# VectorE's sums of weight blocks, tied behind the remainder of the second pair of weights ahead of them

## The chip, the cores and the metric

The kernel runs on one core of a Trainium2 chip. Its time is device microseconds (us) of that core for one execution; the median of several runs counts. In the texts below, PE is TensorE (matmuls), DVE is VectorE, ACT is ScalarE, POOL is GpSimd and SP is SyncE, whose queue issues most of the loads.

## The reference, cut to what matters

Two transformer blocks over 256 rows of 2048 float32 numbers. The first has a mixer (gated linear attention and dilated attention), and then the gated feed-forward layer in which the change lies:

```
h2 = rms_norm(x, norm2_g)
x = x + (silu(h2 @ w_gate) * (h2 @ w_up)) @ w_down      # w_gate, w_up: 2048 x 5632; w_down: 5632 x 2048
```

The second block has retention, a convolution and windowed attention, each with large projections. Nearly all of the work is matmuls of the 256 rows with weight matrices that are read from memory once.

## The kernel before, in words

**Products in three parts.** Each float32 operand is split into a rounded part `hi` (a cast on ACT, line 168) and the remainder `lo` = source - `hi` (a subtraction on DVE, line 169). The helper `split` writes both. A product is then three matmuls (`three`, lines 193 to 195): x hi with w hi, x hi with w lo, x lo with w hi.

**Weights.** `linear` walks over one 512-column slice of a matrix. A `raw` tile holds 2 x 128 rows of it (128 x 1024 numbers, 512 KB), loaded by SP (`rows`, line 126) into one of 5 buffers. `split` makes a *pair* (`hi`, `lo`) of it in one of 4 buffers, and twelve matmuls use the pair. A cast can start when PE is through with the pair four before it; a load can start when the remainder of the raw tile five before it is done.

**The feed-forward layer.** The 5632 hidden columns are 11 slices of 512. Six of them are `plain`: gate product, tanh, up product, then line 562 (DVE) multiplies gate and up, and `act_done` transposes the result on PE (line 551). The other five are computed by `seven`: a 2 x 2 block product with seven multiplications in place of eight. I call each such slice a *block of products*; its work is cut into 28 pieces, which stand in the queue `side`. `deal`, called after each group of three matmuls of a `linear`, takes a piece from that queue every 1.75 groups (the first 12 pieces) or 5.75 groups (the other 16). So the pieces lie between the matmuls of `plain` and `down`.

**The sums.** Each of the last 16 pieces of a block (`rest`) takes four blocks of weights b12, b11, b22, b21 (tiles named `b` or `u`, in a ring of six; loaded by `ahead` one group of four pieces early), makes a sum of two of them in place (a subtraction on DVE, line 676, 128 x 1024), splits the sum into a pair by `parts` and multiplies it by `times` (six matmuls). Five blocks have 80 sums. b12 - b11 is written over b11, b12 - b22 over b12, b22 - (b12 - b11) over b22, and b21 - that over b21.

**What sets the order.** Each engine works through its own queue in order. The order in a queue is made when the program is built, by a scheduler with its own estimate of when each instruction can run (`schedule_with_timeline_sim=True`). Where its estimate has a block of weights landed, it puts the sum into DVE's queue at the first free place.

Of the kernel before, what the change touches and what calls it, by code (L numbers as in the profile page):

```python
# [9 lines left out]
F32 = mybir.dt.float32  # L10
# [3 lines left out]
ALU = mybir.AluOpType  # L14
# [66 lines left out]
def model(ctx, tc, a, out):  # L81
# [12 lines left out]
    V, A, G, T = nc.vector, nc.scalar, nc.gpsimd, nc.tensor  # L94
    cnt = [0]

    def nm(s):
        cnt[0] += 1
        return f"{s}{cnt[0]}"
# [4 lines left out]
    def unit(i, shape, dtype=F32):  # L104
        return wk.tile([P] + list(shape), dtype, tag=f"u{i}", name=nm(f"u{i}_"))
# [15 lines left out]
    def raw_tile():  # L121
        return raw_p.tile([P, 2, 512], F32, tag="raw", name=nm("raw"))

    def rows(dst, w, k, c0, n=512):

        return nc.sync.dma_start(dst[:, :, :n], w[k * P:(k + 2) * P, c0:c0 + n].rearrange("(k p) f -> p k f", p=P))

    def fetch(w, kg, c0, n):

        raws = [raw_tile() for _ in range(2)]  # L130
        for i in range(2):
            rows(raws[i], w, 4 * kg + 2 * i, c0, n)
        return raws
# [29 lines left out]
        G.tensor_tensor(o, ms, nhalf[:, :ms.shape[-1]], ALU.pow)  # L163


    def split(hi, lo, src, scale=None):
        if scale is None:
            A.copy(hi, src)  # L168
            V.tensor_tensor(lo, src, hi.bitcast(F32), ALU.subtract)  # L169
        else:  # L170
            A.activation(hi, src, AF.Copy, scale=scale)
            V.scalar_tensor_tensor(lo, src, scale, hi.bitcast(F32), ALU.mult, ALU.subtract)
# [12 lines left out]
    def deal():  # L185
        if side:
            pace[1] += 1
            if pace[1] >= pace[0]:
                pace[1] -= pace[0]
                side.popleft()()  # L190

    def three(o, xh, xl, hi, lo, start, stop):
        T.matmul(o, xh, hi, start=start, stop=False)  # L193
        T.matmul(o, xh, lo, start=False, stop=False)  # L194
        T.matmul(o, xl, hi, start=False, stop=stop)  # L195

    def linear(w, c0, n, groups, got=(), fine=False):
        accs = [ps_acc.tile([P, 512], F32, tag="acc", name=nm("acc")) for _ in range(2)]
        for gi, ((xh, xl), kg) in enumerate(groups):
            raws = got[gi] if gi < len(got) else fetch(w, kg, c0, n)  # L200
            for k in range(4):
                k2 = k % 2
                if k2 == 0:
                    raw = raws[k // 2]
                    hi = hl_p.tile([P, 2, 512], F32R, tag="hi", name=nm("hi"))
                    lo = hl_p.tile([P, 2, 512], F32R, tag="lo", name=nm("lo"))
                    if fine and gi == 0:
                        for j in range(2):
                            split(hi[:, j, :n], lo[:, j, :n], raw[:, j, :n])
                    else:  # L210
                        split(hi[:, :, :n], lo[:, :, :n], raw[:, :, :n])
                for t in range(2):
                    o = accs[t][:, :n]
                    st, en = gi == 0 and k == 0, gi == len(groups) - 1 and k == 3
                    sl = slice(t * P, (t + 1) * P)
                    three(o, xh[:, k, sl], xl[:, k, sl], hi[:, k2, :n], lo[:, k2, :n], st, en)
                    deal()
        return accs
# [82 lines left out]
    def silu_gate(dst, acc, rh_t):  # L301

        A.activation(dst, acc, AF.Tanh, scale=rh_t)
        V.scalar_tensor_tensor(dst, dst, 1.0, acc, ALU.add, ALU.mult)
# [127 lines left out]
    for vb in range(2):  # L432
# [4 lines left out]
        for hh in range(2):  # L437
# [19 lines left out]
            for t in range(2):  # L457
                o = po[:, t * S:(t + 1) * S]
                T.matmul(o, aT[:, t], v[:, t, vs], start=True, stop=True)
                for c in range(2):  # L460
                    n = 2 * t + c
# [82 lines left out]
    def act_done(j, sg):  # L544
        ah, al = acts[j] = pair(mt_p, "m")
        for i in range(2):
            ps = ps_w.tile([P, 512], F32, tag="w", name=nm("tr"))
            for k in range(2):
                for t in range(2):
                    c = (2 * i + k) * P  # L550
                    T.transpose(ps[:, k * S + t * P:k * S + (t + 1) * P], sg[:, t, c:c + P], ident)
            split(ah[:, 2 * i:2 * i + 2].rearrange("p c s -> p (c s)"),
                  al[:, 2 * i:2 * i + 2].rearrange("p c s -> p (c s)"), ps)
# [50 lines left out]
    def parts(src):  # L604
        hi = hl_p.tile([P, 2, 512], F32R, tag="hi", name=nm("hi"))
        lo = hl_p.tile([P, 2, 512], F32R, tag="lo", name=nm("lo"))
        split(hi, lo, src)
        return hi, lo

    def times(o, which, hl, kp):  # L610
        for j in range(2):
            k = 2 * kp + j
            three(o, *left(which, k), hl[0][:, j], hl[1][:, j], k == 0, k == 7)

    def temp(tag, bufs):
        return sm.tile([P, 512], F32, tag=tag, name=nm("c"), bufs=bufs)
# [3 lines left out]
    def block_tile():  # L620

        i = ring[0] % 6
        ring[0] += 1
        if i < 2:
            return raw_p.tile([P, 2, 512], F32, tag=f"b{i}", name=nm("b"), bufs=1)
        if i < 4:
            return mt_p.tile([P, 2, 512], F32, tag="n" + "hl"[i - 2], name=nm("b"), bufs=1)
        return unit(6 + i, [2, 512])

    def work_bank():  # L630
        return ps_w.tile([P, 512], F32, tag="w", name=nm("at"))

    def seven(j):

        c0 = j * 512
        c = {}

        def first(kp, n):
            if kp == 0:
                c[n] = work_bank()  # L640
            raw = raw_tile()
            rows(raw, (w_gate, w_up, w_gate)[n], (0, 8, 8)[n] + 2 * kp, c0)
            times(c[n], ("A11", "S4", "A12")[n], parts(raw), kp)
            if n == 2:
                ahead(0, kp)
            if kp < 3:
                return
            if n < 2:
                c["p", n] = temp("Lx", 4)
                A.copy(c["p", n], c[n])  # L650
                return
            sg = c["sg"] = unit(5, [2, 512])
            c11 = temp("junk2", 3)
            V.tensor_tensor(c11, c["p", 0], c[2], ALU.add)
            silu_gate(sg[:, 0], c11, rh[:, 0:1])

        def ahead(kp, n):

            if kp > 3:
                return  # L660
            for i in ((0, 1), (), (2,), (3,))[n]:
                b = c["b", kp, i] = block_tile()
                load = rows(b, (w_up, w_gate, w_up, w_gate)[i], (0, 0, 8, 8)[i] + 2 * kp, c0)
                if j == 1 and kp == 0:
                    tc.keep_in_program_order(load)

        def rest(kp, n):
            ahead(kp + 1, n)
            if n == 0:
                if kp == 0:  # L670
                    pace[0] = 5.75
                    c["P"] = [work_bank() for _ in range(3)] + [ps_acc.tile([P, 512], F32, tag="acc", name=nm("acc"))]
            b12, b11, b22, b21 = [c["b", kp, i] for i in range(4)]
            dst, x0, x1, which = ((b11, b12, b11, "S1"), (b12, b22, b12, "S3"), (b22, b22, b11, "S2"),
                                  (b21, b22, b21, "A22"))[n]
            V.tensor_tensor(dst, x0, x1, ALU.subtract)  # L676
            times(c["P"][n], which, parts(dst), kp)
            if kp == 3 and n == 3:
                last()

        def last():
            b5, b7, b6, b4 = c["P"]
            p1, p3, sg = c["p", 0], c["p", 1], c["sg"]
            V.tensor_tensor(p1, p1, b6, ALU.add)
            c12, c21 = temp("junk2", 3), temp("junk2", 3)
            V.tensor_tensor(c12, p1, b5, ALU.add)
            V.tensor_tensor(p1, p1, b7, ALU.add)
            V.tensor_tensor(c21, p1, b4, ALU.subtract)
            V.tensor_tensor(p1, p1, b5, ALU.add)
            V.tensor_tensor(c12, c12, p3, ALU.add)  # L690
            silu_gate(sg[:, 1], c21, rh[:, 1:2])
            for t, cu in enumerate((c12, p1)):
                V.scalar_tensor_tensor(sg[:, t], cu, r2h[:, t:t + 1], sg[:, t], ALU.mult, ALU.mult)
            act_done(j, sg)


        pace[0] = 1.75
        side.extend([lambda kp=kp, n=n: first(kp, n) for kp in range(4) for n in range(2)])
        side.extend([lambda kp=kp: first(kp, 2) for kp in range(4)])
        side.extend([lambda kp=kp, n=n: rest(kp, n) for kp in range(4) for n in range(4)])  # L700

    def drain():
# [369 lines left out]
```

## Time and profile before

| | us |
|---|---|
| median of 3 runs (lowest, highest) | 1926.29 (1925.13, 1928.86) |
| the profiled execution | 1927.01 |
| its span, first to last instruction | 1924.9 |
| PE busy | 1908.3 |
| DVE busy | 1276.6 |
| ACT busy | 969.2 |

A row of the timeline gives the start, the duration, the engine, the line, the operation, out <- in by the program's names, and in brackets how long the engine stood idle before it and what ended that. Ends of matmuls are modelled: a 512-column matmul is shown 0.39 us long, though the next one starts after 0.23 us. The granted clock of PE is 1.00 (2.4 GHz) in all stretches below.

### The profile page before, as it was taken

The numbers are of one execution on the slowest core, as the hardware profiler recorded it, in microseconds if no ns is written. First come the engines' busy times: TensorE is split into PE (matmuls) and PEld (weight loads), VectorE is DVE, ScalarE is ACT, GpSimd is POOL, SyncE is SP. The second block draws the span as 40 slices with busy tenths as digits, with TensorE's granted clock in tenths as the row PEclk, the third lists the DMA queues.
The fourth block names the chain that finished last, engine by engine and source line by source line (L and its number), as shares of the span: only waits on it lengthen the run. The fifth ranks groups of instructions, "written<-read, shape, count | busy, mean of one in ns | idle before, by whom it ended". The sixth has DMA issues, their size and how long they took to land.

```text
span 1924.9 us, 23850 instructions
## 1 busy us (share of the span) xinstructions
PE 1908.3 (99%) x8826; PEld 1569.4 (82%) x8826; DVE 1276.6 (66%) x1489; ACT 969.2 (50%) x1313; POOL 203.8 (11%) x315
## 2 busy tenths in 40 slices
PE   9999999999999999999999999999999999999999
PEld 8877888888888788788788888888888888878787
DVE  5454555586887797788788875554555666677654
ACT  6544545465546455455455454444444354566542
POOL 1000222110000000000000110100000003754100
PEclk9999999999999999999999999999999999999999
DMA  8665665568868678677687656565666556544464
GB/s 276 197 212 148 186 176 167 170 186 265 279 221 275 217 230 270 219 254 252 219 274 248 191 165 189 162 195 169 189 190 189 192 179 187 172 132 132 145 202 135
DMA packets 203012, 387.72 MB, mean 201 GB/s; under 512 B 12344, under 2 KB 21072, under 8 KB 202768
## 3 DMA queue, kind: packets, MB, share of 16 engines
q1 hardware_dynamic: 201472, 381.86, 64.1%
q0 software_dynamic: 992, 4.03, 0.7%
q8 instruction: 69, 1.13, 0.2%
q10 hardware_dynamic: 432, 0.31, 0.1%
q14 instruction: 47, 0.39, 0.1%
HBM read 384.04 MB, written 3.68 MB: 201 GB/s over the span
## 4 chain that ended last, share of the span: by engine, by line
PE 49%; DVE 1%; POOL 1%; issue 0%; DMA 0%; ACT 0%; DVEq 0%; ACTq 0%
PE acc L194 14%; PE acc L193 14%; PE acc L195 14%; PE at L968 1%; PE at L194 1%; PE at L193 1%; PE at L195 1%; DVE lo L169 1%; PE tr L949 0%; PE tr L231 0%; PE at L916 0%; PE at L918 0%; PE at L917 0%; PE tr L313 0%; PE at L774 0%
## 5 line engine op out<-in xcount | busy, mean ns | idle before, releaser
L169 DVE TENSOR_TENSOR lo<-raw,hi 128x1024 fp32r<-128x1024 f32 (+3 forms) x646 | 786.1, 1224 | 472.9 <-ACT hi L168 468.9
L168 ACT CAST hi<-raw 128x1024 fp32r<-128x1024 f32 (+3 forms) x646 | 669.6, 1040 | 668.7 <-PE acc L195 563.8
L194 PE MATMUL acc<-lo,xh 128*128 128x512 f32 (+3 forms) x1640 | 636.6, 388 | 0.4 <-DVE lo L169 0.4
L195 PE MATMUL acc<-hi,xl 128*128 128x512 f32 (+3 forms) x1640 | 636.3, 388 | 0.0
L193 PE MATMUL acc<-hi,xh 128*128 128x512 f32 (+3 forms) x1640 | 622.7, 389 | 2.3 <-ACT hi L168 2.3
L193 PEld LDWEIGHTS acc<-hi,xh 128*128 128x128 f32 x1640 | 307.9, 188 | 66.0 <-issue 4.4
L194 PEld LDWEIGHTS acc<-lo,xh 128*128 128x128 f32 x1640 | 308.6, 188 | 62.9 <-issue 2.5
L195 PEld LDWEIGHTS acc<-hi,xl 128*128 128x128 f32 x1640 | 308.7, 188 | 60.6 <-issue 1.4
L194 PE MATMUL acc<-lo,mh 128*128 128x512 f32 x640 | 251.1, 392 | 0.6 <-DVE lo L169 0.3
L195 PE MATMUL acc<-hi,ml 128*128 128x512 f32 x640 | 248.9, 392 | 0.0
L193 PE MATMUL acc<-hi,mh 128*128 128x512 f32 x640 | 247.1, 393 | 1.5 <-ACT mh L168 1.0
L193 PEld LDWEIGHTS acc<-hi,mh 128*128 128x128 f32 x640 | 120.4, 188 | 27.8 <-DVE x L260 1.9
L194 PEld LDWEIGHTS acc<-lo,mh 128*128 128x128 f32 x640 | 120.2, 188 | 26.6 <-DVE lo L169 2.6
L195 PEld LDWEIGHTS acc<-hi,ml 128*128 128x128 f32 x640 | 119.8, 188 | 24.1
L168 ACT CAST hi<-b 128x1024 fp32r<-128x1024 f32 x54 | 57.0, 1055 | 72.8 <-PE acc L195 49.7
L728 POOL DMA_DIRECT2D u<-in_c_even_dram x1 | 0.6, 633 | 649.6 <-PE at L195 649.6
L169 DVE TENSOR_TENSOR lo<-b,hi 128x1024 fp32r<-128x1024 f32 x54 | 65.9, 1220 | 4.1 <-ACT hi L168 3.6
L676 DVE TENSOR_TENSOR b<-b,b 128x1024 f32<-128x1024 f32 x41 | 50.0, 1222 | 26.4 <-DMA b<-in_w_gate_dram 12.6
L194 PE MATMUL at<-lo,u 128*128 128x512 f32 x160 | 63.2, 395 | 0.3 <-DVE lo L169 0.3
L193 PE MATMUL at<-hi,u 128*128 128x512 f32 x160 | 62.4, 390 | 0.0
L195 PE MATMUL at<-hi,u 128*128 128x512 f32 x160 | 62.4, 390 | 0.0
L260 DVE TENSOR_TENSOR x<-x,acc 128x512 f32<-128x512 f32 x80 | 52.3, 681 | 2.0 <-PE acc L195 1.9
(257 smaller groups left out, 1582.6 us busy)
## 6 DMA issues: line engine op xcount, KB each, us to landing
raw<-in_ev_w_in_dram SPq DMA_DIRECT2D x128, 512.0 KB, 3.9
raw<-in_w_gate_dram SPq DMA_DIRECT2D x88, 512.0 KB, 4.5
raw<-in_w_down_dram SPq DMA_DIRECT2D x88, 512.0 KB, 4.9
raw<-in_w_in_dram SPq DMA_DIRECT2D x80, 512.0 KB, 3.7
raw<-in_od_w_in_dram SPq DMA_DIRECT2D x72, 512.0 KB, 3.7
raw<-in_w_up_dram SPq DMA_DIRECT2D x68, 512.0 KB, 4.6
raw<-in_w_out_dram SPq DMA_DIRECT2D x32, 512.0 KB, 3.8
raw<-in_ev_w_out_dram SPq DMA_DIRECT2D x32, 512.0 KB, 3.6
```

The costliest lines, as they stand in the source:

```text
L168: A.copy(hi, src)
L169: V.tensor_tensor(lo, src, hi.bitcast(F32), ALU.subtract)
L193: T.matmul(o, xh, hi, start=start, stop=False)
L194: T.matmul(o, xh, lo, start=False, stop=False)
L195: T.matmul(o, xl, hi, start=False, stop=stop)
L260: V.tensor_tensor(xs, xs, accs[t], ALU.add)
L676: V.tensor_tensor(dst, x0, x1, ALU.subtract)
L728: nc.gpsimd.dma_start(ce, a["c_even"][:, :512])
L968: T.matmul(pv[e * 64:(e + 1) * 64, :S], vo[:, k, g * 64:(g + 1) * 64], PT[:, :, e], start=k == 0, stop=k == t)
```

## The change: an order edge per sum

`split` can note the instruction of the remainder in a list of the last eight, and does so for the pairs of `linear` and of `parts`. When a sum is written, the last entry of that list is the pair just ahead of it in the program, and `rests[-2]` the one before that. The sum gets an order edge behind that remainder, without a signal (`NoSync`), since both are on DVE.

```
+    rests = deque(maxlen=8)
+
-    def split(hi, lo, src, scale=None):
+    def split(hi, lo, src, scale=None, note=False):
         if scale is None:
             A.copy(hi, src)
-            V.tensor_tensor(lo, src, hi.bitcast(F32), ALU.subtract)
+            rest = V.tensor_tensor(lo, src, hi.bitcast(F32), ALU.subtract)
+            if note:
+                rests.append(rest)
...
-                        split(hi[:, :, :n], lo[:, :, :n], raw[:, :, :n])
+                        split(hi[:, :, :n], lo[:, :, :n], raw[:, :, :n], note=True)
...
     def parts(src):
...
-        split(hi, lo, src)
+        split(hi, lo, src, note=True)
...
-            V.tensor_tensor(dst, x0, x1, ALU.subtract)
+
+            tc.add_manual_dep(V.tensor_tensor(dst, x0, x1, ALU.subtract).ins, rests[-2].ins.name,
+                              mybir.DependencyInfo(mybir.DependencyClass.NoSync, mybir.DependencyReason.DATA),
+                              reason="order")
```

The scheduler then orders the queues anew. Lines below the edit carry higher numbers in the changed kernel: 169 is 171, 260 is 264, 562 is 566, 676 is 681.

DVE in the second block of products, at the end of an up product of `plain`. `lo` rows are remainders (of weights, `raw`, or of a sum, `b` or `u`), L676 is a sum and L562 the product of gate and up. Before:

```order
L169 TENSOR_TENSOR lo_5377<-u_1074_5216,hi_5376 128x1024
L169 TENSOR_TENSOR lo_5414<-raw_5409,hi_5413 128x1024
L169 TENSOR_TENSOR lo_5430<-raw_5410,hi_5429 128x1024
L676 TENSOR_TENSOR u_1120_5438<-u_1119_5436,u_1120_5438 128x1024
L562 SCALAR_TENSOR_TENSOR u_1062_5160<-acc_5165,r2h_3455,u_1062_5160 128x512
L562 SCALAR_TENSOR_TENSOR u_1062_5160<-acc_5166,r2h_3455,u_1062_5160 128x512
L169 TENSOR_TENSOR lo_5442<-b_5261,hi_5441 128x1024
```

The same place in the changed kernel:

```order
L171 TENSOR_TENSOR lo_5377<-u_1074_5216,hi_5376 128x1024
L171 TENSOR_TENSOR lo_5414<-raw_5409,hi_5413 128x1024
L681 TENSOR_TENSOR b_5261<-b_5259,b_5261 128x1024
L171 TENSOR_TENSOR lo_5430<-raw_5410,hi_5429 128x1024
L566 SCALAR_TENSOR_TENSOR u_1062_5160<-acc_5165,r2h_3455,u_1062_5160 128x512
L566 SCALAR_TENSOR_TENSOR u_1062_5160<-acc_5166,r2h_3455,u_1062_5160 128x512
L171 TENSOR_TENSOR lo_5442<-b_5261,hi_5441 128x1024
```

The sum of u_1120 has left its place ahead of the two products; the sum of b_5261, which stood 12 rows ahead of lo_5430, is now just ahead of it.

DVE, the first sum of the second block of products (u_1026). Before, it stood in the last stretch of the first block, between that block's remainders:

```order
L169 TENSOR_TENSOR lo_4563<-raw_4558,hi_4562 128x1024
L676 TENSOR_TENSOR u_1026_5011<-u_1025_5009,u_1026_5011 128x1024
L169 TENSOR_TENSOR lo_4580<-b_4423,hi_4579 128x1024
L169 TENSOR_TENSOR lo_4590<-raw_4559,hi_4589 128x1024
L169 TENSOR_TENSOR lo_4614<-raw_4609,hi_4613 128x1024
```

In the changed kernel:

```order
L171 TENSOR_TENSOR lo_5048<-raw_5045,hi_5047 128x1024
L171 TENSOR_TENSOR lo_5060<-raw_5014,hi_5059 128x1024
L681 TENSOR_TENSOR u_1026_5011<-u_1025_5009,u_1026_5011 128x1024
L171 TENSOR_TENSOR lo_5069<-raw_5066,hi_5068 128x1024
L171 TENSOR_TENSOR lo_5101<-u_1026_5011,hi_5100 128x1024
```

It moved some 50 rows down, to two remainders ahead of its own (lo_5101).

SP's queue in the second block: b_5373 is the fourth block of weights (b21) of a group, raw tiles are weights for `linear`. Before:

```order
L126 DMA b_5373<-in_w_gate_dram 128x2x512
L126 DMA raw_5410<-in_w_down_dram 128x2x512
L126 DMA b_5341<-in_w_up_dram 128x2x512
L126 DMA raw_5460<-in_w_down_dram 128x2x512
L126 DMA raw_5461<-in_w_down_dram 128x2x512
```

In the changed kernel:

```order
L126 DMA raw_5410<-in_w_down_dram 128x2x512
L126 DMA b_5341<-in_w_up_dram 128x2x512
L126 DMA raw_5460<-in_w_down_dram 128x2x512
L126 DMA b_5373<-in_w_gate_dram 128x2x512
L126 DMA raw_5461<-in_w_down_dram 128x2x512
```

The load of b_5373 went behind three others.

## Rows read from the trace of the kernel before

**Rows 1.** The page, part 1: engine, busy us, share of span, instructions.

```profile
PE 1908.3 (99%) x8826; PEld 1569.4 (82%) x8826; DVE 1276.6 (66%) x1489; ACT 969.2 (50%) x1313; POOL 203.8 (11%) x315
```

**Rows 2.** Busy time by stretch: all of the sums, and 46 us without waits.

```profile
core 0: us, PE busy (x) PEld busy (x) DVE busy (x) ACT busy (x) POOL busy (x), PEclk, DMA share, GB/s
430.00:1070.00 640.00, 633.61 (x2814) 518.72 (x2813) 517.20 (x505) 340.10 (x349) 0.00 (x0) 1.00 0.75 245
576.00:622.00 46.00, 46.00 (x209) 38.04 (x208) 35.81 (x36) 28.17 (x30) 0.00 (x0) 1.00 0.82 263
```

**Rows 3.** What PE waited for, 430 to 1070: total us, times, longest.

```profile
PE tr L551 <- DVE u L562: 4.9, 3, 2.5
PE acc L193 <- DVE x L260: 0.6, 1, 0.6
PE at L194 <- DVE lo L169: 0.3, 1, 0.3
PE acc L194 <- DVE lo L169: 0.3, 1, 0.3
```

**Rows 4.** Timeline of PE around 660.

```profile
657.87 0.39 PE L195 MATMUL acc<-hi,ml 128*128 128x512 f32 x1
658.09 0.39 PE L193 MATMUL at<-hi,u 128*128 128x512 f32 x1
660.97 0.33 PE L551 MATMUL tr<-cm,u 128*128 128x128 f32 x1 [2.49 <-DVE u L562]
```

**Rows 5.** Timeline of DVE, 645 to 663.

```profile
645.88 2.49 DVE L676 TENSOR_TENSOR b<-b,b 128x1024 f32<-128x1024 f32 x2 [3.26 <-DMA b<-in_w_up_dram]
...
652.82 2.35 DVE L169 TENSOR_TENSOR lo<-raw,hi 128x1024 fp32r<-128x1024 f32 x2
659.02 1.23 DVE L676 TENSOR_TENSOR u<-u,u 128x1024 f32<-128x1024 f32 x1 [3.85 <-DMA u<-in_w_gate_dram]
660.16 1.41 DVE L562 SCALAR_TENSOR_TENSOR u<-acc,r2h,u 128x512 f32<-128x512 f32 x2
661.48 1.22 DVE L169 TENSOR_TENSOR lo<-b,hi 128x1024 fp32r<-128x1024 f32 x1
```

**Rows 6.** Line 676: duration min/median/max, and its idle time by transfer (us, times).

```profile
L676 DVE TENSOR_TENSOR b<-b,b x41: 1216/1220/1228, 473.6 to 1061.6; 128x1024 f32<-128x1024 f32 x41
...
  DMA b<-in_w_up_dram: 23.8, 12
  DMA b<-in_w_gate_dram: 12.6, 8
  DMA u<-in_w_gate_dram: 10.2, 5
  DMA u<-in_w_up_dram: 9.7, 6
```

**Rows 7.** Timeline of DVE: the first sum of the second block.

```profile
548.65 1.23 DVE L676 TENSOR_TENSOR u<-u,u 128x1024 f32<-128x1024 f32 x1 [1.66 <-DMA u<-in_w_gate_dram]
```

**Rows 8.** Timelines of DVE, ACT and PE: that sum's cast, what stands around it.

```profile
607.88 2.36 DVE L169 TENSOR_TENSOR lo<-raw,hi 128x1024 fp32r<-128x1024 f32 x2 [0.36 <-ACT hi L168]
...
611.53 1.06 ACT L168 CAST hi<-u 128x1024 fp32r<-128x1024 f32 x1 [0.30 <-PE at L195]
...
615.64 0.39 PE L193 MATMUL at<-hi,u 128*128 128x512 f32 x1
```

**Rows 9.** Timelines of DVE and PE around 955: a small gap.

```profile
953.18 1.23 DVE L676 TENSOR_TENSOR u<-b,u 128x1024 f32<-128x1024 f32 x1 [3.33 <-DMA b<-in_w_up_dram]
954.32 1.22 DVE L169 TENSOR_TENSOR lo<-raw,hi 128x1024 fp32r<-128x1024 f32 x1
...
954.83 0.61 PE L193 MATMUL acc<-hi,mh 128*128 128x512 f32 x2
955.60 0.50 PE L194 MATMUL acc<-lo,mh 128*128 128x512 f32 x1
```

**Rows 10.** Timelines of ACT and PE: a cast with little cover.

```profile
662.73 1.06 ACT L168 CAST hi<-b 128x1024 fp32r<-128x1024 f32 x1 [6.10 <-DVE lo L169]
...
665.38 0.40 PE L193 MATMUL at<-hi,u 128*128 128x512 f32 x1
```

**Rows 11.** SP's waits, and a load of blocks (KB, us to landing), 430 to 1075.

```profile
SPq L126 <- DVE lo L169: 508.3, 293, 7.1
...
b<-in_w_gate_dram SPq DMA_DIRECT2D x27, 512.0 KB, 4.5
```

## The prediction

> **What bounds the kernel now.** I read the engines' busy shares first. TensorE (PE) is busy for 99% of the span and VectorE (DVE) for 66% [rows 1]. PE's matmuls are therefore the time, and a change that touches only VectorE's order can win or lose what PE stands idle and no more. All sums of line 676 lie between 443 and 1063 us, so the second view is the busy time of 430 to 1070: PE is busy for 633.6 of 640 us [rows 2]. Third, the list of what PE waited for there: 4.9 us in three waits of the transposes of line 551 for VectorE's L562, and three single ones of 0.6, 0.3 and 0.3 us [rows 3], 6.1 us in six waits.
>
> A listed wait is a little shorter than what it costs. A 512-column matmul is drawn 0.39 us long, but the next one starts 0.22 to 0.23 us after it. At 658.09 a matmul starts, and the transposition behind it at 660.97 [rows 4]: 2.88 us where 0.23 is usual, so 2.65 is lost against 2.49 listed, 0.16 more. Six waits then cost 6.1 + 6 x 0.16 = 7.1 us. A gap under 0.39 is not listed at all: two matmuls start at 954.83 and 0.23 later, the next one at 955.60 [rows 9], 0.3 us lost. I count two such gaps, 0.6. **PE loses 7.7 us in this stretch.**
>
> Where they come from is seen on VectorE's timeline before 660.97 [rows 5]. Its remainders end at 652.82 + 2.35 = 655.17. The next instruction is a sum of line 676 whose block of weights has not landed; it starts 3.85 us later, at 659.02. Behind it stand the two products of line 562, which had nothing to wait for but their place, and PE's transposition needs the first of them. The other two waits of line 551 have the same sum in front. VectorE as a whole stood 56.3 us in 31 waits of sums for a transfer [rows 6], of which PE felt under 8: elsewhere PE has remainders in stock.
>
> **What the change does, part by part.** No instruction is added or removed. 80 sums of 1.22 us (98 us of VectorE) move back, each to just behind the remainder of the second pair ahead. The edge joins two instructions of one engine, so it adds no signal between engines.
>
> *The wait for the transfer.* The first sum of the second block ran at 548.65, after 1.66 us of waiting [rows 7]; its cast started at 611.53 [rows 8], 63 us later. The sum that waited until 645.88 [rows 5] has its cast, found by the order of the queues, at 662.73 [rows 10]. Its new place is behind the remainder that runs at 661.48 (some 5 us earlier without the stall), still 10 us after its data are there. In the order, the first sums of a block of products move some 50 rows of VectorE's queue, the others some 10 to 14. So I expect nearly all of the 56.3 us of VectorE's waits to go.
>
> *The three stalls.* In the second block, the sum before L562 goes and another one, whose data landed long ago, stands one remainder earlier. VectorE is then through its remainders at 655.17 + 1.22 = 656.39 at the latest, and through both products (1.41 us, [rows 5]) at 657.8. The transposition could start at 658.09 + 0.23 = 658.32. So it is met with 0.5 us to spare, and what is next is PE's own stream. That gives back 4.9 + 3 x 0.16 = 5.4 us.
>
> *The small gaps,* 7.7 - 5.4 = 2.3 us. The sum at 953.18 waited 3.33 us, and the remainder behind it came late for PE [rows 9]. It belongs to the next block of products and moves out of this crowded end. I expect these to go too, but new ones of their size may open; I leave half, 1.1 us.
>
> *The cost: the sum now stands on the way to the cast.* In a calm place, the remainder two ahead ends at 607.88 + 2.36 = 610.24, and the cast starts at 611.53, when PE frees its buffer [rows 8]. A sum of 1.23 us put between ends at about 611.45, before that. PE first uses this cast at 615.64, 3.05 us after its end. In the tightest place that I found, the remainder two ahead ends at 662.70 and the cast starts at once, at 662.73 [rows 5, 10]; the sum would push it 1.3 us, and PE uses it 1.59 us after its end. Both are covered, so I take zero. If no cover held, 80 x 1.22 = 98 us would be lost; if it holds everywhere, nothing, and the gain is 7.7. The measured covers of 3.05 and 1.59 against 1.3 put it at the near end.
>
> *The loads.* The fourth block of each group is loaded into the tile that the third sum frees, which now comes later, and SyncE's queue has that load two or three places later. SyncE is waiting most of the time (508 us of 645, for remainders, [rows 11]), so a load that waits for a sum would hold the weights behind it. The third sum stands ahead of the remainder that frees the next buffer of weights, so the load is free no later than what follows it, and its own sum stands some 20 VectorE instructions of up to 1.22 us on, about 20 us against 4.5 us of landing [rows 11]. Cost zero; if that cover were gone, each of some 20 loads would hold the weights behind it by one VectorE instruction, 20 x 1.22 = 24 us at most.
> The Trainium skill (DMA: Bandwidth & Descriptors, Anatomy of one DMA) says that a transfer's semaphore wait happens on the issuing sequencer before dispatch, which speaks against moving a freeing sum back. The trace agrees that SyncE is held by remainders; by the rule alone, the loss would be those 24 us.
>
> On PE itself, some 180 of 8343 rows shift by a few places, with the same matmuls; on ScalarE four tanh change places with a cast.
>
> **The sum.** The profiled execution took 1927.0 us (span 1924.9 and 2.1 around it), 0.7 over the median 1926.29 of the runs. 5.4 + 2.3 - 1.1 = 6.6 us less gives 1920.4 for that execution, and 1919.7 against the median.
>
> **Rivals.**
> *The sum is late for the cast (slower).* One mechanism: VectorE runs behind in the dense half of a block, so the remainder two ahead ends one instruction (1.22 us) later than before; the sum then ends too late, the cast slips by 1.3 + 1.22 = 2.5 us, and PE waits 2.5 - 1.59 = 0.9 us at each of 8 sums in 5 blocks, 36 us. With the three stalls gone, 1926.3 - 5.4 + 36 = 1957. It decides from the point where that remainder ends over 0.3 us later than in [rows 5]. For it: VectorE is busy 517 of 640 us [rows 2]. Against: its 56 us of waiting go, and the sums leave the crowded end.
> *The wait is only handed on (same).* The first product meets another wait, such as the sum that now stands one remainder ahead of it, or PE stalls somewhere else; about 3 of the 7.7 stay won: 1923.3. For it: the margin at 658.32 is only 0.5 us.
> *It doesn't do what it says (same).* The freed tiles come later, so the loads do, and the sums go on waiting: 1926.3. Against it are the 10 us between landing and new place.
> *More room than the idle shows (faster).* Weight loads are busy 518.7 of 640 us (81.1%), and 38.04 of 46 (82.7%) in a stretch without waits [rows 2]. By that measure 640 x (1 - 81.1/82.7) = 12.8 us are lost. Returned in full: 1913.5. Against: the transpositions load for a shorter time, and stay.
> The Trainium skill (Perfetto Trace Analysis, Identifying the Most-Contended Engine) says that matmul busy time is a poor measure of the room left and the weight loads' share a better one; by that rule this rival would be the forecast.
>
> **How the numbers follow.** Forecast 0.62, sum late 0.08, handed on 0.22, doesn't do it 0.05, more room 0.03. A measurement of this kernel can tell about 0.2% (3.9 us) from no change. The forecast's own range is 1918 to 1922.5 (all of 7.7 won, or half of it). Ranging to the two cases of no change gives 1917 to 1926.5; the slow end and the far fast end stay out, some 0.13. Faster: most of the forecast, the room, and a little of the handed on, 0.67. Same: 0.23. Slower: 0.08 and 0.02 for small losses, 0.10.
>
> **What would show it.** Right: in the list of VectorE's waits, sums waiting for transfers fall from 56 us to under 10; PE's waits between 430 and 1065 hold no line 551 for the products, and their total is under 2 us; VectorE's busy time is unchanged; casts of sums now wait for VectorE's sum in places, without PE waiting behind them. Wrong: PE waits for a cast or remainder of a sum, in several blocks at the same place; or SyncE waits for a sum for long; or the products wait behind the sum a remainder ahead.

## The result, and the profile after

| us | before | after |
|---|---|---|
| median (lowest, highest), 5 runs each | 1925.94 (1925.13, 1928.86) | 1915.58 (1915.46, 1916.15) |
| the profiled execution | 1927.01 | 1915.46 |
| its span | 1924.9 | 1913.7 |

The ratio is 0.9944, with a 95% interval of 0.9934 to 0.9955: faster, by 10.4 us. The forecast was 1919.7, and the time lies 1.4 us below the range. The direction came as forecast, and so did the fall of VectorE's waits; the forecast gain was too small, 6.6 us where 10.4 came.

The engines' busy shares after, against [rows 1]:

```profile
PE 1903.8 (99%) x8826; PEld 1570.2 (82%) x8826; DVE 1278.3 (67%) x1489; ACT 969.6 (51%) x1313; POOL 205.3 (11%) x315
```

VectorE does the same work, 1278.3 for 1276.6 us. The stretch of the sums after, in the columns of [rows 2]:

```profile
430.00:1070.00 640.00, 639.23 (x2855) 527.78 (x2855) 524.76 (x509) 343.40 (x353) 1.18 (x2) 1.00 0.77 248
```

PE is busy for 639.23 of 640 us, where it was 633.61. What it still waits for there, against the four lines of [rows 3]:

```profile
PE tr L555 <- DVE ml L171: 0.8, 4, 0.2
```

The transpositions (line 551, now 555) no longer wait for products, and no cast or remainder is late. VectorE's list of waits in the same stretch:

```profile
DVE lo L171 <- ACT hi L170: 111.7, 132, 2.6
DVE c L691 <- PE at L199: 0.7, 4, 0.2
```

No transfer is in it; before, sums waited 56.3 us for transfers [rows 6]. VectorE now waits where it should, for casts. ScalarE's and then SyncE's lines that name a sum (681 is the old 676), with SyncE's largest, which answers to [rows 11]:

```profile
ACT hi L170 <- DVE b L681: 7.2, 7, 1.4
...
ACT hi L170 <- DVE u L681: 2.4, 2, 1.3
```

```profile
SPq L126 <- DVE lo L171: 456.8, 258, 6.2
SPq L126 <- DVE b L681: 32.2, 25, 2.6
SPq L126 <- DVE u L681: 16.0, 12, 2.5
```

Nine casts wait for a sum, and SyncE waits 48 us for sums; PE feels neither. VectorE's timeline after, at the place of [rows 5]:

```profile
649.42 1.22 DVE L681 TENSOR_TENSOR b<-b,b 128x1024 f32<-128x1024 f32 x1
650.55 1.22 DVE L171 TENSOR_TENSOR lo<-raw,hi 128x1024 fp32r<-128x1024 f32 x1
651.69 1.40 DVE L566 SCALAR_TENSOR_TENSOR u<-acc,r2h,u 128x512 f32<-128x512 f32 x2
...
659.55 1.22 DVE L681 TENSOR_TENSOR b<-b,b 128x1024 f32<-128x1024 f32 x1
660.68 0.69 DVE L171 TENSOR_TENSOR ml<-tr,mh 128x512 fp32r<-128x512 f32 x1
...
669.65 1.22 DVE L681 TENSOR_TENSOR u<-u,u 128x1024 f32<-128x1024 f32 x1
```

The sum that had waited until 659.02 runs at 669.65. The products (line 566) start at 651.69, where they started at 660.16. (This trace is 2.0 us ahead from its first 34 us on, which is none of the change's doing, as told below.) The sum at 659.55 stands ahead of the remainder `ml` of the transposed product, and that makes the one kind of gap that is left, on PE's timeline after:

```profile
660.84 0.39 PE L197 MATMUL acc<-hi,mh 128*128 128x512 f32 x1
661.42 0.66 PE L555 MATMUL tr<-cm,u 128*128 128x128 f32 x4 [0.19 <-DVE ml L171]
```

0.58 us from start to start where 0.23 is usual: 0.35 lost, at 661, 789, 916 and 1044, 1.4 in all.

**Where the difference lies.** All 8826 matmuls are recorded in both traces, so their starts can be set side by side by their number in order. I call the time from the start of matmul 1900 (402 us) to that of matmul 5000 (1106 us in the trace before) *the stretch*: 703.8 us before, 694.5 after, 9.3 less. Behind it the two run alike, 814.4 us each. Another 2.0 us lie ahead of matmul 150, in the first 34 us, where the change moves nothing. There, in the windows of before and then of after (columns as in [rows 2]):

```profile
12.00:16.00 4.00, 3.17 (x12) 2.83 (x13) 3.63 (x7) 3.60 (x8) 0.00 (x0) 0.81 1.07 372
16.00:20.00 4.00, 4.00 (x20) 3.98 (x18) 3.83 (x7) 3.61 (x8) 0.00 (x0) 0.77 1.05 369
```

```profile
12.00:16.00 4.00, 3.61 (x18) 3.27 (x19) 3.87 (x7) 3.61 (x7) 0.00 (x0) 1.00 1.08 373
16.00:20.00 4.00, 4.00 (x24) 4.00 (x24) 3.86 (x7) 3.61 (x8) 0.00 (x0) 1.00 1.05 381
```

The profiled execution of before was granted 0.81 and 0.77 of PE's clock there, that is, the lower level (1.2 GHz) for part of it, after PE had stood idle for 1.71 us at 12.43. After had 1.00 throughout. A second profile of the kernel before (below) had 1.00 as well, so this is chance of one execution.

### The profile page after: what moved, and what is told of

Read it like the earlier page. It is cut to its first block, busy times and chain, and to the rows that moved or that the text cites. A ratio compares the mean times of both kernels' runs of the same rounds, so it can differ in the third digit from the quotient of the medians.

```text
span 1913.7 us, 23825 instructions
## 1 busy us (share of the span) xinstructions
PE 1903.8 (99%) x8826; PEld 1570.2 (82%) x8826; DVE 1278.3 (67%) x1489; ACT 969.6 (51%) x1313; POOL 205.3 (11%) x315
## 4 chain that ended last, share of the span: by engine, by line
PE 97%; DVE 1%; POOL 1%; ACT 0%; DMA 0%; issue 0%; SPq 0%; DVEq 0%; ACTq 0%
PE acc L199 27%; PE acc L198 27%; PE acc L197 27%; PE at L197 3%; PE at L199 3%; PE at L198 3%; PE at L975 1%; PE tr L235 1%; PE tr L317 1%; PE tr L555 0%; PE tr L956 0%; PE at L923 0%; DMA xT<-in_x_t_dram 0%; ACT hi L170 0%; PE at L925 0%; PE at L924 0%
```

## Experiments

In all, "first profile" is the one of before that stands ahead of the prediction. Each run has its own runs of the kernel before beside it; their medians were 1927.74 (the last, first, later and product edges), 1927.66 (the fourth, one block, GpSimd) and 1926.98 (the rest). DVE's waits are the sum of its lines for sums waiting for transfers, 430 to 1070.

| kernel | median us | ratio to before | stretch us | DVE's waits us |
|---|---|---|---|---|
| before, first profile | 1925.94 | | 703.8 | 56.3 |
| before, second profile | 1927.57 (1 run) | | 706.1 | 61.1 |
| after | 1915.58 | 0.9944 (0.9934 to 0.9955) | 694.5 | 0 |
| `rests[-1]` | 1917.67 | 0.9951 (0.9938 to 0.9963) | 696.0 | 0 |
| `rests[-3]` | 1914.39 | 0.9934 (0.9921 to 0.9946) | 693.1 | 0 |
| `rests[-4]` | 1915.77 | 0.9944 (0.9932 to 0.9957) | 695.0 | 0 |
| 20 first sums of groups | 1916.92 | 0.9952 (0.9939 to 0.9964) | 695.1 | 25.5 |
| the other 60 | 1916.43 | 0.9947 (0.9934 to 0.9961) | 695.5 | 5.6 |
| behind products | 1918.43 | 0.9954 (0.9942 to 0.9967) | 696.8 | 15.6 |
| one block | 1925.66 | 0.9992 (0.9983 to 1.0001) | 705.6 | 53.6 |
| block loads by GpSimd | 1955.22 | 1.0153 (1.0139 to 1.0167) | 732.6 | 82.6 |
| before, 2 Lx | 1960.66 | 1.0170 (1.0156 to 1.0184) | 706.5 | 60.7 |
| before, 2 Lx, 6 raw | 1956.92 | 1.0153 (1.0139 to 1.0167) | 703.1 | 63.2 |
| after, 2 Lx, 6 raw | 1945.79 | 1.0097 (1.0083 to 1.0111) | 694.9 | 0 |

**The last remainder.** The edge leads to the pair just ahead, so each sum has less time to its cast.

```
-rests[-2].ins.name
+rests[-1].ins.name
```

> The order edge goes behind the remainder of the pair just ahead (rests[-1]) in place of the second pair ahead, so every sum is one pair later. Theory 1 (PE's waits, each with what follows it, were the whole loss; a sum costs nothing while its cast is covered): at the calm place the sum would end near 613.7 of the trace of before and its cast near 614.9, still ahead of PE's use at 615.64, but in the dense half of a block the cover of 1.59 us is gone; PE then waits for casts or remainders of sums at a few places in each block, 0.3 to 0.6 us each, together some 5 us: about 1921, between the two kernels. Rival (being late costs nothing, since PE has stock enough): within 1 us of the changed kernel, 1915 to 1917. Rival (late sums set the pace): slower than before, over 1928.

Measured: 1.4 us longer in the stretch than after. ScalarE's waits for sums, 430 to 1070:

```profile
ACT hi L170 <- DVE b L681: 111.2, 49, 3.6
ACT hi L170 <- DVE u L681: 59.6, 24, 3.6
```

Now 73 of 80 casts wait for their sums, 171 us in all, and PE loses 1.5 us at six gaps: five of 0.49 to 0.50 us from start to start, one per block (they end at 551.17 to 1061.68), and one of 0.44. The four gaps of after are gone, so the 1.4 us are a balance. Theory 1 had about 1921, its first rival at most 1917; 1917.67 is close to the rival. So even the tightest edge is not slower than before, and nearly everywhere the cast has time to spare, beyond the two places that the prediction measured.

**The first sums of the groups, and the others.** Is each stall the doing of the sum in front of it, so that the gain divides among the sums?

```
+            if kp == 0:          # the 20; the other kernel has: if kp > 0 (the 60)
                 tc.add_manual_dep(...)
```

> The order edge is given only to the four sums of the first group of each block (20 of 80), those that stood in the crowded end of the block before. Theory 1 (VectorE held by sums that wait for transfers): the three stalls of the transpositions stay, since a sum of the last group causes them; gone are the small waits near 565, 575, 829, 838, 956 and 959, 2.0 us and 0.14 us each of slower matmuls behind them: 2.9 us, about 1923. Rival (the gain comes from taking 20 sums of 1.22 us out of the crowded end, not from waits): most of the 9 to 10 us, 1919 or less.

> The order edge is given to the sums of the second to fourth group of each block (60 of 80); those of the first group stay where the scheduler puts them. Theory 1: the three stalls of the transpositions go (5.8 us with the slower matmuls behind them) and the small waits that sums of later groups cause (1.8 us), together 7.6: about 1918.3; the small waits at the ends of blocks stay, 2.9 us. Rival (the crowded end is what matters): 3 us or less, 1923 or more.

Measured: against the first profile the 20 alone win 8.7 us of the stretch, the 60 alone 8.3, and all 80 win 9.3. The parts don't add up, and the account by single sums fails. The rival of the crowded end had the 20 right (1919 or less) and the 60 wrong: 1916.43 where it had 1923 or more. VectorE's timeline with the 20 tied, where [rows 5] had its long wait; the sum of u_1120 is not tied here:

```profile
651.20 0.74 DVE L566 SCALAR_TENSOR_TENSOR u<-acc,r2h,u 128x512 f32<-128x512 f32 x1
654.28 1.23 DVE L681 TENSOR_TENSOR u<-u,u 128x1024 f32<-128x1024 f32 x1 [2.34 <-DMA u<-in_w_gate_dram]
655.42 0.75 DVE L566 SCALAR_TENSOR_TENSOR u<-acc,r2h,u 128x512 f32<-128x512 f32 x1
```

It still stands ahead of a product and waits 2.34 us for its block, and PE has no stall there: the whole queue is earlier. Nor is it alone: with the 20 tied, 56 sums keep their place in VectorE's queue to within two, and their waits for transfers still fall, from 40.8 us in the first profile (45.8 in the second) to 25.1. SyncE's issue of that sum's load, in the trace before, with the 20 tied, and after:

```profile
652.93 0.37 SPq L126 DMA_DIRECT2D u<-in_w_gate_dram  x1
```

```profile
648.89 0.37 SPq L126 DMA_DIRECT2D u<-in_w_gate_dram  x1
```

```profile
645.67 0.37 SPq L126 DMA_DIRECT2D u<-in_w_gate_dram  x1
```

The load goes out 4.0 and 7.3 us earlier; counted from matmul 1900 of each trace (402.27, 401.18 and 400.30), which takes out the unlike starts, 3.0 and 5.3. I read it so: a waiting sum holds the remainders behind it, these hold SyncE's loads, and the next sum waits again, so that VectorE's lateness is handed from sum to sum. Breaking the row at some sums frees the others.

**Behind the products alone.** Each sum goes behind the last product of line 566 written ahead of it, and behind no remainder.

```
-            tc.add_manual_dep(..., rests[-2].ins.name, ...)
+            if gated:
+                tc.add_manual_dep(total.ins, gated[-1].ins.name, ...)
```

> No edge behind a remainder: each sum gets one behind the last product of gate and up (line 562 of before) that stands ahead of it in the program, so that these products never stand behind a waiting sum; all other sums stay early. Theory 1: the three stalls go, 5.4 us and some 0.4 of slower matmuls behind them, while VectorE's waits for transfers stay at 45 us or more: about 1920.5. Rival (the wait is only handed on, to the remainders behind the products): gain under 2.5 us, 1923.5 or more, with PE waiting for a remainder of a sum at the same three places.

Measured: 7.0 us of the stretch, and VectorE's waits fall to 15.6 us, where theory 1 had 45 or more. But the edge reached further than was expected: 37 of the 80 sums stand 2 to 12 places later in VectorE's queue than before. These waited 36.3 us in the first profile and wait for nothing here; the other 43 waited 20.0 us and wait 15.5. Most of the fall is thus the edges' own doing, and this run says little on handing on.

**Before, once more.** Unchanged, for a second profile.

> The kernel before, unchanged, profiled once more. In its first profile TensorE was granted 0.77 to 0.81 of its clock between 12 and 20 us, and it was 2.0 us behind the changed kernel from there to the start of the sums at 443, where both run the same instructions. If that was chance, this profile shows clock 1.00 there and a span near 1923, and 2 us of the 11 between the two profiles are none of the change's. If it belongs to the kernel, it shows the dip again and a span near 1925. In the stretch of the sums both readings expect the same three stalls of the transpositions and VectorE's waits for transfers at 50 to 60 us.

The stretch from 12 to 20 us had the full clock, as the reading by chance had it, though the span was 1925.6 us and not near 1923, since the stretch of the sums was longer. PE's list for 430 to 1070, against [rows 3]:

```profile
PE tr L551 <- DVE u L562: 6.1, 4, 1.8
PE at L194 <- DVE lo L169: 1.3, 3, 0.5
...
```

That stretch took 706.1 us, 2.3 more than in the first profile, with a fourth stall of the transpositions. The kernel before varies here from one execution to the next: its 38 timed runs go from 1924.1 to 1931.9, those of after from 1915.5 to 1916.2.

**One block.** Only the four first sums of the second block are tied.

```
+            if kp == 0 and j == 3:
                 tc.add_manual_dep(...)
```

> The order edge only for the four sums of the first group of the second block (4 of 80), which the kernel before runs at the end of the first block. Theory F, with waits that feed themselves within one block: the end of the first block and the second block lose what the changed kernel saved there, 4.4 us between matmuls 2400 and 3450 of the trace, and the third to fifth block keep their waits and their stalls near 790 and 919: about 1922 where before is 1926. Rival (the schedule of before is unlucky as a whole and any nudge frees it): 8 us or more, stalls gone in all blocks. Rival (waits are local to the sum that waits): under 2 us, since the stall near 661 comes from a sum of the last group, which stays where it is.

Measured: no difference that is clear of the noise. The second block wins 2.5 us against the second profile (matmul 2400 to 3150: 168.6 for 171.1), and the third gives 2.45 back within 70 us (3150 to 3450: 69.80 for 67.35). Both lie outside what the kernel before shows by itself: its two profiles and the control with two Lx (below), in the same order there, have 171.1 to 173.5 and 67.3 to 67.5. There VectorE, and then PE, show:

```profile
688.25 1.22 DVE L681 TENSOR_TENSOR b<-u,b 128x1024 f32<-128x1024 f32 x1 [3.95 <-DMA u<-in_w_up_dram]
```

```profile
690.66 0.50 PE L198 MATMUL at<-lo,u 128*128 128x512 f32 x1 [0.17 <-DVE lo L171]
692.93 0.50 PE L198 MATMUL acc<-lo,mh 128*128 128x512 f32 x1 [0.82 <-DVE lo L171]
```

In the second block the untied sums wait 5.9 us (10.1 to 12.0 in the two profiles of before), in the third 14.1 (11.1 and 12.1). A queue that arrives earlier only waits longer at the next untied sum. So what is won at one place is lost at the next unless that one is tied too.

**Loads of blocks by GpSimd.** To take the blocks out of SyncE's queue, so that no remainder holds them.

```
+load = rows(b, ..., queue=nc.gpsimd)   # in ahead(), the kernel before
```

> The kernel before with one change: the loads of the sums' blocks are issued by GpSimd's queue, idle in this stretch, in place of SyncE's, where they stand behind loads of weights that wait for VectorE's remainders. No edges; sums stay as early as the scheduler puts them. Theory F (the waits feed themselves: a sum that waits holds remainders, these free the buffers for which SyncE's queue stands still, so the next sum's load is late): VectorE's waits for transfers fall from 56 us to under 20, the three stalls shrink to under 2 us in total, about 1918. Rival (the sums simply stand ahead of what their own loads can reach, whatever the queue): waits stay at 40 us or more, 1923 or more.

Measured: the opposite, 27.6 us slower. VectorE waits 82.6 us for blocks, and PE's list (430 to 1070) begins:

```profile
PE acc L194 <- DVE lo L169: 8.8, 11, 2.3
PE at L194 <- DVE lo L169: 5.6, 4, 1.9
```

The loads land 4.8 to 5.0 us after their issue by the medians, much as SyncE's do. But the scheduler also put the first five sums 18 to 35 places earlier in VectorE's queue, and PE's clock falls in the stretch (below). More than one thing changed, so this run says nothing on the path through SyncE's queue.

**Six buffers of raw weights.** Which way is the lateness handed on: through the loads of the weights, or of the blocks? With a sixth raw buffer each load of weights stands a place earlier in SyncE's queue, and the loads of blocks stay behind the same remainder. Room for it comes from Lx (2 buffers for 4), which costs some 32 us behind the stretch (846.2 for 814.4 from matmul 5000 to the end, where 6 us in all were expected); so only stretches are compared.

```
-raw_p ... bufs=5      -tag="Lx" ... bufs=4
+raw_p ... bufs=6      +tag="Lx" ... bufs=2    (the control: Lx alone)
```

> The kernel before with two buffers instead of four for the tile Lx, which makes room for the next run; the order of the instructions changes only behind the stretch of the sums. All theories: in the stretch as before, VectorE waiting 50 to 65 us for transfers of blocks and TensorE losing 9 to 12 us against the changed kernel; total within 6 us of before.

> The same with six buffers of raw weights instead of five. Each load of weights for a pair moves a place earlier in SyncE's queue; the loads of blocks keep their place behind the same remainder of VectorE. Theory F1 (a late remainder holds SyncE's queue, so that the next loads of blocks are late and VectorE waits again): VectorE's waits for blocks stay at 45 to 65 us, and TensorE's stretch is won back by under 3 of the 9 us. Theory F2 (a late remainder makes the loads of the weights late, so that their casts and remainders are late for TensorE): the waits of sums may stay, but with the deeper stock of weights TensorE's stretch is won back by 5 us or more.

> The changed kernel with six buffers of raw weights and two of Lx. F1 and F2: nothing is left to be won in the stretch, so it is as long as in the changed kernel, to 0.7 us, with no wait of VectorE for a block. If a deeper stock of weights is worth something by itself, the four remaining gaps before the transpositions go and the stretch is about 1.4 us shorter.

Measured: 706.5 us in the control, 703.1 with six buffers: 3.4 of the 12.0 us between the control and after. One profile each does not settle that, since three executions in the order of before took 703.8, 706.1 and 706.5 us there. The timed runs do better: 1954.94 to 1958.27 with six buffers, 1958.75 to 1961.98 in the control, 3.7 us between the medians of the whole kernel. PE's list with six buffers, and then in the control:

```profile
PE tr L551 <- DVE u L562: 3.0, 4, 1.2
PE at L194 <- DVE lo L169: 1.4, 4, 0.7
```

```profile
PE tr L551 <- DVE u L562: 5.6, 4, 1.8
PE at L194 <- DVE lo L169: 1.1, 3, 0.5
```

VectorE's waits for blocks stay (63.2 for 60.7), as F1 had it, but some 3 to 4 us are won, between its 3 and the 5 of F2. So one more buffer of weights takes away about a quarter of the loss; whether more buffers would take more was not tried. That the rest runs through the loads of the blocks is what the issue times above show in one place, but no run took that path away alone. In the changed kernel the sixth buffer wins nothing (694.9 for 694.5): no wait there is for weights.

**The third and the fourth remainder.** `rests[-3]` and `rests[-4]` in place of `rests[-2]`.

> The edge behind the remainder of the fourth pair ahead (rests[-4]): sums two pairs earlier than in the changed kernel, still after their data. What PE lost in the changed kernel's stretch is four gaps of 0.35 us at the transpositions and the slower matmuls behind them, some 2 us. If these come from sums that are late for a dense place, this version takes up to 1.5 us off: about 1914.5. If they come from the order of PE's own queue: the same as the changed kernel, 1915.5 to 1917, and sums that wait for transfers may be back with 5 to 10 us.

> The edge behind the remainder of the third pair ahead (rests[-3]). With the last one the late casts cost 1.9 us and with the fourth nothing was late; the second is the changed kernel. All theories: no wait of VectorE for a block, and a time between the changed kernel and the fourth, 1915.3 to 1916.5 where before is 1926 to 1928 (ratio 0.994).

(The 1.9 us named there for the last remainder is a line of its whole span; in the stretch it loses what is told above.) Measured: the fourth is as fast as after, with gaps of its own, four of 0.40 us and one of 0.63 from start to start. The third was expected between the two and is faster than both, 1914.06 to 1915.32 in five runs where after had 1915.46 to 1916.15. The ratios to before overlap, but its stretch is 1.4 us shorter, which is what after lost at its four gaps. Its window, and VectorE at the place of after's gap:

```profile
430.00:1070.00 640.00, 640.00 (x2861) 529.42 (x2860) 526.43 (x510) 345.30 (x354) 3.30 (x6) 1.00 0.78 249
```

```profile
658.28 1.22 DVE L681 TENSOR_TENSOR b<-b,b 128x1024 f32<-128x1024 f32 x1
659.41 0.69 DVE L171 TENSOR_TENSOR ml<-tr,mh 128x512 fp32r<-128x512 f32 x1
```

The sum is done one place earlier, `ml` starts at 659.41 where it started at 660.68, and PE is busy for all of the 640 us. No gap over 0.42 us from start to start is left among the sums.

## Why the gain was larger than forecast

**The step that failed is "PE loses 7.7 us in this stretch".** With `rests[-3]` PE waits for nothing in the list, so I take the difference to it as what the first profile really lost: 703.8 - 693.1 = 10.7 us, where the prediction's sum had 7.7. By the distance from one matmul's start to the next, and against the same distances with `rests[-3]`, it divides so. Eight more distances over 0.42 us lose 7.6 us: these are the six waits and two gaps that the prediction counted, at the right size. Twenty more of 0.26 to 0.42 us, where 0.227 is usual, lose 2.15. Of the rest, 0.7 is spread over 2937 distances of 227.34 ns on average where they are 227.10 (no run shows why), and 0.2 over the short ones. The twenty are of two kinds. Eight are small waits by themselves, 0.8 us. Twelve, of 0.33 to 0.34 us, follow directly on a late matmul and lose 1.3, as behind the gap of [rows 9] on PE's timeline of before:

```profile
955.93 0.39 PE L195 MATMUL acc<-hi,ml 128*128 128x512 f32 x1
956.16 0.40 PE L194 MATMUL acc<-lo,mh 128*128 128x512 f32 x1
956.40 0.39 PE L195 MATMUL acc<-hi,ml 128*128 128x512 f32 x1
956.63 0.40 PE L193 MATMUL acc<-hi,mh 128*128 128x512 f32 x1
```

The matmul that had waited starts at 955.60; the next one comes 0.33 us later, and then 0.23, 0.24, 0.23. So a wait goes on costing some 0.1 us after it has ended, and small waits that the list does not show were there in number. The list of waits gave 6.1 of 10.7. With 10.7 in place of 7.7, and the 1.4 that stayed in place of 1.1, the prediction's own sum becomes 9.3 us, the difference of the two stretches.

**The execution was not the median's in its parts.** The prediction set its sum against the profile's 1927.0, 0.7 over the median. That total held two deviations which nearly cancelled: 1.6 us of slow start against the second profile (matmul 150 at 33.98 and 32.35 us), and a stretch 2.3 us shorter than the second profile's. In that one the loss was 706.1 - 693.1 = 12.9 us by the unrounded starts. After's 694.5 is 9.3 us below the first and 11.5 below the second by the unrounded starts, and the 10.4 of the medians lies between. How long the stretch was in the timed runs is not on record, so the step from 9.3 to 10.4 is argued: the waits that the change takes away are what varies in the kernel before.

**The wait for the transfer: right.** 56.3 us to none, "nearly all" as forecast. (By the two traces the first five sums of a later block move 42 to 47 places in VectorE's queue and the others 7 to 13, somewhat less than the 50 and the 10 to 14 of the prediction.)

**The three stalls: right in that they go, in part for another reason.** The products are no longer behind a waiting sum; but with the 20 sums tied the sum is still there, still waits, and the stall is gone all the same, since VectorE comes earlier. So the place alone did not make the stalls; VectorE's lateness there was part of it.

**The small gaps: right.** Half of 2.3, 1.1 us, were to stay as new ones; 1.4 stayed, by a sum ahead of `ml`.

**The sum on the way to the cast: right,** zero. The rival with 36 us of loss at eight sums in each block is refuted at the forecast's edge, where nine casts wait, and at the tighter one, where 73 do.

**The loads: right,** zero. SyncE is held 48 us by sums and 457 by remainders, 505 in place of 508. The Trainium skill (DMA: Bandwidth & Descriptors, Anatomy of one DMA), in a section on transfers issued by GpSimd, says of DMA engines as such that the wait for a semaphore happens on the issuing sequencer. So it shows here, on SyncE. The waits cost nothing that PE's list shows, as the loads had time in hand: that of 645.67 has its sum at 669.65.

**The rivals.** "Handed on" and "doesn't do it" are out: no line of PE's list took the stalls' place beyond 0.8 us. "More room than the idle shows", to which I gave 0.03, was the nearest in time: weight loads were busy for 81.1% of the stretch, are now for 527.78 / 640 = 82.5%, and with `rests[-3]` for 529.42 / 640 = 82.7%, just the share of the 46 us without waits [rows 2]. Its 12.8 us (12.7 from the unrounded times) were read from the execution that lost 10.7; the second profile's share, 516.78 / 640 = 80.7%, gives some 15 where 12.9 were lost. So it was 2 us too high in both, where the list of waits was 4.6 too low in the first. My reason against it, that transpositions load for a shorter time, was not weighed in numbers. The Trainium skill (Perfetto Trace Analysis, Identifying the Most-Contended Engine) prefers the weight loads' share to the matmuls' busy time; the traces agree that it comes nearer, 12.7 us against the 6.4 that PE was not busy [rows 2].

**What stays open.** By which of SyncE's loads most of the lateness is handed on: a sixth buffer of raw weights wins some 3 to 4 of 12.0 us, and the run that was to test the rest changed too much. It is open too why the other matmuls of before are 0.24 ns further apart on average.

## What to carry to other kernels

Where the bounding engine is 99% busy, take its room from the distance between starts, or from the share of its weight loads against a stretch without waits (here 2 us too high), and not from the list of its waits alone: here the list showed 6.1 of 10.7 us. Before a change that removes waits, take two profiles: where waits feed one another, one execution does not show how much the usual one loses. An instruction that waits for a transfer in a queue that others need should go behind the point where its data have landed, with some room left to its own user: of the four edges the third was best, the last cost some 3 us more in the stretch. It needs doing wherever the row of waits starts anew: tying a few in one block only moved the wait to the next, tying 20 of 80 over all blocks won 8.7 of the 9.3 us.

## What the runs showed of the hardware

In the first profile, nine distances over 0.35 us end at a 512-column matmul, and behind each of these the next matmul starts 0.33 to 0.34 us later, where 0.23 is usual. The other three end at a transposition; the 0.31 us that follow two places on are there with `rests[-3]` as well, where nothing waited (behind the matmul of 661.77).

PE's granted clock fell after some stalls and not after others. With the blocks' loads on GpSimd it fell behind four of PE's six longest waits (2.31, 2.19, 2.04 and 1.85 us), and not behind the other two (2.13 and 1.86). PE's timeline at the first, and the window that follows:

```profile
504.91 0.50 PE L194 MATMUL acc<-lo,xh 128*128 128x512 f32 x1 [2.19 <-DVE lo L169]
```

```profile
506.00:509.00 3.00, 3.00 (x9) 2.35 (x8) 3.00 (x3) 0.00 (x0) 0.72 (x1) 0.51 0.87 210
```

That is half the clock (1.2 GHz), with matmuls 0.427 us apart. In the first profile of before, 2.49 us of waiting [rows 4] had no such sequel; 1.71 us at the start had one, and so had 1.48 in the control with two Lx, where 0.85 and 1.07 at the same place in other executions had none.

A 512 KB load issued by GpSimd landed in 4.8 to 5.0 us by the medians of its kinds, no later than SyncE's 4.7 to 5.3 in the same run.
